# A two-layer decoder trunk with a product-key expert stage: 16 more tokens take gathered expert rows, and the gates come from one product

## The chip, the cores and the metric

The kernel runs on one core of one Trainium2 chip. The metric is device time in microseconds (us) of one launch. The engines are TensorE (PE, with its weight loads PEld), VectorE (DVE), ScalarE (ACT), GpSimd (POOL) and SyncE (SP), and 16 DMA engines move data.

## The reference

Two layers (`DEPTH = 2`), 512 tokens of width 1024, all float32. Each layer has a token mixer (retention beside a gated linear recurrence), cross-attention into 256 memory tokens, and an expert stage, here called PEER; a final norm closes it. The change touches the expert stage alone, which is:

```python
def _peer(x, g_ffn, w_pq, sub_k1, sub_k2, peer_u, peer_v):
    hf = _rmsnorm(x, g_ffn).reshape(N, D)
    q = (hf @ w_pq).reshape(N, PEER_HEADS, PEER_KEY_DIM)
    ...
    v1, i1 = lax.top_k(s1, K)
    v2, i2 = lax.top_k(s2, K)
    cand = (v1[..., :, None] + v2[..., None, :]).reshape(N, PEER_HEADS, K * K)
    vals, ci = lax.top_k(cand, K)
    ...
    idx = (e1 * PEER_KEYS + e2).reshape(N, PEER_HEADS * K)
    gates = jax.nn.softmax(vals, axis=-1).reshape(N, PEER_HEADS * K)
    ...
    ub = jnp.take(peer_u, ib, axis=0)
    act = jax.nn.gelu(jnp.einsum('tkd,td->tk', ub, xb).astype(jnp.float32))
    vb = jnp.take(peer_v, ib, axis=0)
    out = jnp.einsum('tk,tkd->td', (gb * act).astype(vb.dtype), vb)
```

Eight heads pick 16 experts each, so a token uses 128 of the 16,384 experts. An expert is a row of `peer_u` and a row of `peer_v`, 1024 numbers each.

## The kernel before, in words

**Two ways to do an expert.** Of the 512 tokens, the first `TD = 384` are done densely: all 16,384 experts are computed for them, in `NK = 128` units of 128 experts, and a gate that is zero for the experts not chosen selects. The last 128 tokens, one per partition, are done by rows: for each of the 128 places k of a token's list, a gather (an indirect DMA on POOL) brings 128 rows of 1024, one per partition.

**Products.** A float32 product is made of three float32r products of split halves (`mm3`): the weight w is cast by ACT to its high part `wh` (L200), DVE subtracts to get the low part `wl` (L202). `pull` and `weights` keep two weights ahead; `w` has 4 buffers, `wh` and `wl` 3. The weights of all stages come in one order, so the first weight of the next layer's mixer follows V's last one.

**Stages of an expert layer.** First queries and keys (`keys`, `top16`): DVE finds the best 16 of each half, and L853 turns each index into a number `idf`. Then **U**: unit j multiplies `peer_u`'s weight with the tokens (24 matmuls of 384 columns, L216 to L218), ACT applies gelu into `ag`, and SP stores `acts`. Three generators are fed between the units, each by a credit: `routes` (route by route in the order `RORD`: candidates, top 16, look-ups L905 and L907, softmax), `scatter` (gates), and `rows_u` (the gathered rows of U, with `XPACE` per unit). `scatter` spreads the gates of four tokens at a time over all 128 x 128 experts: DVE makes one-hot rows, ACT scales them, PE multiplies. Two of four groups use split halves (256 columns, L963, then a copy and DVE's addition L967), two a plain float32 product (128 columns, L971). `rows_u` multiplies each gathered row with `hrow` on DVE and sums along it (L782).

Then **V**: for unit j, `wv` = activation times gate (L1066), split into `ws` (L222, L223), and 24 products into eight accumulators `out`, one bank each, which are held for the whole stage. Units run in groups of 8 from the last group to the first (`v_order`); the last two units of the last group (j = 6 and 7) are held back. `rest` first finishes `rows_u`, then runs `rows_v`: gather into `rv` (4 buffers, L795), then DVE adds it, times `wrow`, to `yrow` (L800). It gets a credit of `VPACE = 1.75` per unit against 1.3 per gather, and whatever is left runs behind the last unit. At the end, for each of the eight accumulators, L1080 adds `yrow` transposed, then the two held units are added, and L1084 adds the result to `x`.

Each engine runs its instructions in program order, as the kernel's scheduler has arranged them; a waiting instruction holds up all those behind it on its engine.

Of the kernel before, what the change touches and what calls it, by code (L numbers as in the profile page):

```python
# [19 lines left out]
D = 1024  # L20
T = 512
# [12 lines left out]
TD = 384  # L34
# [4 lines left out]
GVN = 2  # L39
# [3 lines left out]
RORD = [*range(TD // 128, TT), *range(TD // 128)]  # L43
# [14 lines left out]
XPACE = 0.8  # L58
# [95 lines left out]
def trunk(ctx: ExitStack, tc: tile.TileContext, A, out, dbg=None):  # L154
# [107 lines left out]
    nc.scalar.copy(identr, ident)  # L262

# [497 lines left out]
    def peer(l):  # L761
        acts = dram.tile([NK // GRP, 128, GRP, TD], F32, name=f"acts{l}")
        gd = dram.tile([NK // GRP, 128, NTB, GRP, TB], F32, name=f"gates{l}")
        NG = T // 128 - TD // 128
        left = ExitStack()
        gp = left.enter_context(tpool(name=f"pg{l}", bufs=1))
        if NG:
            hrow = gp.tile([128, D], F32, name="hrow")
            arow = gp.tile([128, 128], F32, name="arow")
            grow = gp.tile([128, 128], F32, name="grow")  # L770
            irow = gp.tile([128, 2, 128], I32, name="irow")
            wrow = gp.tile([128, 128], F32, name="wrow")
# [3 lines left out]
        def rows_u():  # L776
            for k in range(PH * K):
                r = gp.tile([128, D], F32, name="rows", bufs=3)
                nc.gpsimd.indirect_dma_start(out=r, out_offset=None, in_=A["peer_ur"].rearrange("l e d -> (l e) d"),  # L779
                                             in_offset=bass.IndirectOffsetOnAxis(ap=irow[:, 0, k:k + 1], axis=0))  # L780
                s = gp.tile([128, D], F32, name="prod", bufs=1)
                nc.vector.scalar_tensor_tensor(s, r, 1.0, hrow, op0=OP.mult, op1=OP.mult, accum_out=arow[:, k:k + 1])  # L782
                yield 1.3
                if k % 32 == 31:
                    ks = slice(k - 31, k + 1)
                    nc.scalar.activation(wrow[:, ks], arow[:, ks], AF.Gelu_apprx_tanh)
                    nc.vector.tensor_mul(wrow[:, ks], wrow[:, ks], grow[:, ks])

        def rows_v(vp):
            yrow = vp.tile([128, D], F32, name="yrow")  # L790
            ysum.append(yrow)
            pv = A["peer_v"].rearrange("l j n d -> (l j n) d")
            for k in range(PH * K):
                r = vp.tile([128, D], F32, name="rv", bufs=RVB)
                nc.gpsimd.indirect_dma_start(out=r, out_offset=None, in_=pv,  # L795
                                             in_offset=bass.IndirectOffsetOnAxis(ap=irow[:, 1, k:k + 1], axis=0))
                if k == 0:
                    nc.vector.tensor_scalar(yrow, r, wrow[:, k:k + 1], None, op0=OP.mult)
                else:
                    nc.vector.scalar_tensor_tensor(yrow, r, wrow[:, k:k + 1], yrow, op0=OP.mult, op1=OP.add)  # L800
                yield 1.3
# [8 lines left out]
        with tpool(name=f"pr{l}", bufs=1) as rt, tpool(name=f"ph{l}", bufs=1) as hp, tpool(name=f"pps{l}", bufs=4, space=PS) as psum, \  # L810
# [14 lines left out]
            def token_rows():  # L825
                for c0 in range(0, DC, 4):
                    tr = psm.tile([128, 4, 128], F32, name="sm")
                    for i in range(4):
                        for k in range(2):
                            nc.tensor.matmul(tr[:, i], lhsT=h[c0 + i][:, 1 - k, TD:T], rhs=identr, start=k == 0,  # L830
                                             stop=k == 1)
                    nc.scalar.copy(hrow[:, c0 * 128:(c0 + 4) * 128], tr.rearrange("p c i -> p (c i)"))
# [8 lines left out]
            with tpool(name=f"pk{l}", bufs=1) as kp:  # L841
                def keys(hd, i, q, sk):
# [6 lines left out]
                    for t in range(TT):  # L849
                        wk = kp.tile([128, NK], F32, name="wk", bufs=2)  # L850
                        idx = kp.tile([128, K], U32, name="idx", bufs=2)
                        top16(val[i][t][:, hd], idx, s[:, t], wk)
                        nc.vector.scalar_tensor_tensor(idf[i][t][:, hd], idx, (NK if i == 0 else 1.0) / IDS,  # L853
                                                       C("first") if i == 0 else C("iota")[:, 0:K],
                                                       op0=OP.mult, op1=OP.add)

                for c in range(2 * PH):
# [12 lines left out]
                    if c == 3 and NG:  # L870
                        token_rows()
                drain()

# [4 lines left out]
            def route(t):  # L878
# [3 lines left out]
                ohs = [big[:, o:o + K * NC_].rearrange("p (k c) -> p k c", k=K)  # L882
                       for o in (2 * PH * NC_, 2 * PH * NC_ + K * NC_)]
# [19 lines left out]
                for hd in range(PH):  # L903
                    oh = ohs[hd % 2]
                    nc.vector.tensor_sub(oh, cid[:, hd, None, :].to_broadcast([128, K, NC_]),  # L905
                                         cf[:, hd, :, None].to_broadcast([128, K, NC_]))
                    nc.vector.tensor_reduce(ee[:, hd], oh, axis=AX.X, op=OP.min, apply_absolute_value=True)  # L907
                    yield 1.8
# [15 lines left out]
                if t * 128 >= TD:  # L924
                    nc.vector.tensor_copy(grow, ex[:, 2])
                    base = float(l * NK * NK)
                    nc.vector.tensor_scalar(irow[:, 0], ee.rearrange("p h k -> p (h k)"), IDS, base, op0=OP.mult,  # L927
                                            op1=OP.add)
# [239 lines left out]
```

## Time and profile before

| | us |
| --- | --- |
| median of 3 runs | 3853.55 |
| lowest and highest run | 3851.89, 3855.34 |
| the profiled execution | 3855.28 |
| its span (first to last instruction) | 3853.2 |
| PE busy in the span | 3801.3 (99%) |
| DVE busy | 2999.6 (78%) |
| ACT busy | 1900.1 (49%) |
| POOL busy | 734.3 (19%) |
| moved by DMA | 877.06 MB |

The span is the profiled execution without what lies around it (2.1 us). Busy time of PE counts matmuls as they overlap in the pipeline, so its share says that PE had work, not that it ran at its peak. The mean granted clock of PE was 0.995. In layer 1 the U stage runs from about 808 to 1390 us, V from there to 1917 us.

### The profile page before, as it was taken

To read this page: it belongs to the slowest core of one execution; us is meant where nothing else is said; L and a number is where in the kernel's file an instruction comes from. 1 tells how busy PE (TensorE), PEld (TensorE's weight loads), DVE (VectorE), ACT (ScalarE), POOL (GpSimd) and SP (SyncE) were. 2 spreads that over 40 slices of the span, in tenths; PEclk is the share of its full clock that TensorE was granted. 3 is DMA by queue.
4 is the path that set the end of the run, shared out by engine and by line. 5 is a ranking of instruction groups with operands and counts; after the bars stand their busy time and mean duration, and the time that the engine had idled before them with its cause. 6 is when DMAs were issued, how large, how long until landed. Compare 5 with 4: busy or idle time off the path is not lost.

```text
span 3853.2 us, 56299 instructions
## 1 busy us (share of the span) xinstructions
PE 3801.3 (99%) x20636; PEld 3535.2 (92%) x20636; DVE 2999.6 (78%) x5556; ACT 1900.1 (49%) x3531; POOL 734.3 (19%) x517
## 2 busy tenths in 40 slices
PE   8999999999999999999999999999999999999998
PEld 7888888899999999999978888878999999999998
DVE  7449665999989968777854596659999898687877
ACT  5336444336778843333343363543367788333333
POOL 0000000013233323333200000000232333233432
PEclk9999999999999999999999999999999999999999
DMA  4222342268999989999722223322689999899995
GB/s 150 82 87 95 104 134 69 83 208 317 309 319 348 335 325 338 345 346 346 269 82 77 93 94 104 131 67 88 232 308 312 319 350 315 332 348 342 345 346 213
DMA packets 313476, 877.06 MB, mean 228 GB/s; under 512 B 24945, under 2 KB 131569, under 8 KB 305265
## 3 DMA queue, kind: packets, MB, share of 16 engines
q1 hardware_dynamic: 239472, 605.01, 44.3%
q0 software_dynamic: 73728, 268.47, 19.8%
q8 instruction: 162, 2.65, 0.3%
q14 instruction: 114, 0.93, 0.1%
HBM read 776.13 MB, written 97.26 MB: 227 GB/s over the span
## 4 chain that ended last, share of the span: by engine, by line
PE 88%; DVE 8%; DMA 2%; issue 1%; ACT 1%; POOL 0%; SPq 0%; DVEq 0%; ACTq 0%; POOLq 0%
PE acc L216 18%; PE acc L218 18%; PE acc L217 18%; PE out L216 9%; PE out L217 9%; PE out L218 9%; PE sm L971 2%; DVE wl L202 2%; DMA rows<-peer_ur,irow 1%; PE sm L963 1%; DVE wk L837 1%; DVE idx L839 1%; DVE idx L836 1%; DVE val L838 1%; DVE val L835 1%
## 5 line engine op out<-in xcount | busy, mean ns | idle before, releaser
L200 ACT CAST wh<-w 128x1024 fp32r<-128x1024 f32 x768 | 802.0, 1049 | 1028.0 <-PE acc L217 662.7
L202 DVE TENSOR_TENSOR wl<-w,wh 128x1024 fp32r<-128x1024 f32 x768 | 935.1, 1218 | 338.9 <-ACT wh L200 315.5
L779 POOL DMA_INDIRECT rows<-peer_ur,irow x256 | 360.9, 1410 | 2354.9 <-DVE irow L927 1687.6
L216 PE MATMUL acc<-hf,wh 128*128 128x384 f32 (+1 forms) x2256 | 777.2, 344 | 7.3 <-DVE hf L223 6.1
L218 PE MATMUL acc<-hf,wl 128*128 128x384 f32 (+1 forms) x2256 | 775.9, 345 | 5.9 <-DVE wl L202 5.8
L217 PE MATMUL acc<-hf,wh 128*128 128x384 f32 (+1 forms) x2256 | 774.0, 343 | 0.0
L216 PE MATMUL out<-ws,wh 128*128 128x384 f32 x2048 | 687.6, 336 | 6.3 <-DVE ws L223 6.3
L217 PE MATMUL out<-ws,wh 128*128 128x384 f32 x2048 | 685.9, 335 | 0.0
L218 PE MATMUL out<-ws,wl 128*128 128x384 f32 x2048 | 575.8, 335 | 0.0
L216 PE MATMUL acc<-a,wh 128*128 128x512 f32 x1280 | 507.4, 397 | 15.9 <-ACT wh L200 10.5
L795 POOL DMA_INDIRECT rv<-peer_v,irow x256 | 373.0, 1457 | 716.6 <-DVE yrow L800 609.7
L217 PE MATMUL acc<-a,wh 128*128 128x512 f32 x1280 | 505.1, 395 | 0.0
L218 PE MATMUL acc<-a,wl 128*128 128x512 f32 x1280 | 503.8, 394 | 0.1
L216 PEld LDWEIGHTS acc<-hf,wh 128*128 128x128 f32 x2256 | 425.4, 189 | 17.9 <-DVE hf L223 8.7
L218 PEld LDWEIGHTS acc<-hf,wl 128*128 128x128 f32 x2256 | 425.1, 189 | 17.2 <-DVE wl L202 8.8
L217 PEld LDWEIGHTS acc<-hf,wh 128*128 128x128 f32 x2256 | 425.4, 189 | 7.8
L222 ACT CAST ws<-wv 128x384 fp32r<-128x384 f32 x256 | 131.1, 512 | 537.8 <-PE out L218 268.9
L216 PEld LDWEIGHTS out<-ws,wh 128*128 128x128 f32 x2048 | 385.8, 188 | 6.9 <-DVE ws L223 6.9
L217 PEld LDWEIGHTS out<-ws,wh 128*128 128x128 f32 x2048 | 385.7, 188 | 0.0
L953 ACT ACTIVATE ob<-oab,pg 128x128 fp32r<-128x128 f32 (+1 forms) x1152 | 357.2, 393 | 38.6 <-DVE oab L947 37.7
L218 PEld LDWEIGHTS out<-ws,wl 128*128 128x128 f32 x2048 | 375.9, 188 | 0.0
L800 DVE SCALAR_TENSOR_TENSOR yrow<-rv,wrow,yrow 128x1024 f32<-128x1024 f32 x254 | 324.5, 1278 | 50.9 <-DMA rv<-peer_v,irow 50.9
(291 smaller groups left out, 5186.5 us busy)
## 6 DMA issues: line engine op xcount, KB each, us to landing
w<-peer_u SPq DMA_DIRECT2D x256, 512.0 KB, 5.8
w<-peer_v SPq DMA_DIRECT2D x256, 512.0 KB, 6.3
gates<-stage SPq DMA_DIRECT2D x48, 1024.0 KB, 8.6
gg<-gates SPq DMA_DIRECT2D x30, 1536.0 KB, 9.0
acts<-ag SPq DMA_DIRECT2D x56, 768.0 KB, 6.2
ar<-acts SPq DMA_DIRECT2D x28, 1536.0 KB, 13.7
w<-w_f SPq DMA_DIRECT2D x80, 512.0 KB, 3.3
w<-w_t SPq DMA_DIRECT2D x32, 512.0 KB, 3.3
```

The source lines that it names most:

```text
L200: nc.scalar.copy(wh, w)
L202: nc.vector.tensor_sub(wl, w, wh.bitcast(F32))
L216: nc.tensor.matmul(acc, lhsT=lh, rhs=rl, start=start, stop=False)
L217: nc.tensor.matmul(acc, lhsT=lh, rhs=rh, start=False, stop=False)
L218: nc.tensor.matmul(acc, lhsT=ll, rhs=rh, start=False, stop=stop)
L222: nc.scalar.copy(dst[:, 0], src)
L779: nc.gpsimd.indirect_dma_start(out=r, out_offset=None, in_=A["peer_ur"].rearrange("l e d -> (l e) d"), in_offset=bass.IndirectOffsetOnAxis ...
L795: nc.gpsimd.indirect_dma_start(out=r, out_offset=None, in_=pv, in_offset=bass.IndirectOffsetOnAxis(ap=irow[:, 1, k:k + 1], axis=0))
L800: nc.vector.scalar_tensor_tensor(yrow, r, wrow[:, k:k + 1], yrow, op0=OP.mult, op1=OP.add)
L835: nc.vector.max(v[:, 0:8], src)
L953: nc.scalar.activation(ob[:, i, k % 2], oh[:, 2 * i + 1].bitcast(F32), AF.Copy, scale=pg[:, k, t0 + i:t0 + i + 1])
L971: nc.tensor.matmul(g[:, i], lhsT=oh[:, 2 * i], rhs=ob[:, i, 0], start=True, stop=True)
```

## The change

**Tokens.** `TX = 16`: the dense tokens are 368, and tokens 368 to 383 join the gathered ones. These 16 are held eight times over the 128 partitions, partition 16 g + e holding token e for the heads' part g, so that 16 more gathers of 128 rows in U and 16 in V do their 128 experts each. A product with `pick` replicates their routes, `half` selects each partition's own 16 places, token rows are replicated by ACT copies (`hx`) and transposed by 16 products per layer, and at the end a product with `fold` (16 columns) sums the eight copies. So `hrow`, `arow`, `grow`, `irow`, `wrow`, `yrow` become pairs, and `rows_u` and `rows_v` go over 128 and then 16 places.

**Gates.** `GVN = 0`: all groups of four tokens use the plain float32 product.

**Order and batches.** Routes go in the order 3, 2, 0, 1 (before 3, 0, 1, 2), and gates in 2, 0, 1; `XPACE` goes from 0.8 to 1.3. The index conversions are done by `numbers(t)`, two instructions for a route instead of one for each key and head. Look-ups take two heads at a time. In V, `wv` and `ws` are made for two units at once (736 columns). `rows_u` writes its product in place.

```diff
 TB = 16
-TD = 384
+TX = 16
+TD = 384 - TX
+NX = 128 // TX
...
-GVN = 2
+GVN = 0
...
-RORD = [*range(TD // 128, TT), *range(TD // 128)]
+RORD = [3, 2, 0, 1]
...
-XPACE = 0.8
+XPACE = 1.3
...
+    fold = keep.tile([128, TX], F32, name="fold")
+    nc.vector.tensor_reduce(fold, ident.rearrange("p (g e) -> p e g", g=NX), axis=AX.X, op=OP.add)
+    half = keep.tile([128, 2], F32, name="half")
...
+    pick = keep.tile([128, NX, TX], F32, name="pick")
...
         def rows_u():
...
+            for i, n in enumerate((PH * K, TX)):
+                while not routed[RORD[i]]:
+                    yield
+                for k in range(n):
+                    r = gp.tile([128, D], F32, name="rows", bufs=3)
...
         def rows_v(vp):
...
+            for i, n in enumerate((PH * K, TX)):
+                yrow = vp.tile([128, D], F32, name=f"yrow{i}")
+                ysum.append(yrow)
+                for k in range(n):
+                    r = vp.tile([128, D], F32, name="rv", bufs=RVB)
...
-                        top16(val[i][t][:, hd], idx, s[:, t], wk)
-                        nc.vector.scalar_tensor_tensor(idf[i][t][:, hd], idx, (NK if i == 0 else 1.0) / IDS,
-                                                       C("first") if i == 0 else C("iota")[:, 0:K],
-                                                       op0=OP.mult, op1=OP.add)
+                        top16(val[i][t][:, hd], idf[i][t][:, hd].bitcast(U32), s[:, t], wk)
...
-                for hd in range(PH):
-                    oh = ohs[hd % 2]
...
+                for hd in range(0, PH, 2):
+                    nc.vector.tensor_sub(oh, cid[:, hd:hd + 2, None, :].to_broadcast([128, 2, K, NC_]),
+                                         cf[:, hd:hd + 2, :, None].to_broadcast([128, 2, K, NC_]))
...
+                if t == RORD[1]:
+                    rep = psm.tile([128, 3, PH * K], F32, name="sm")
+                    nc.tensor.matmul(rep.rearrange("p i k -> p (i k)"), lhsT=pick.rearrange("p g e -> p (g e)"),
+                                     rhs=ex.rearrange("p i k -> p (i k)"), start=True, stop=True)
...
+                    nc.vector.tensor_copy(grow[1], own[:, 2])
+                    places(irow[1], own[:, 0], own[:, 1])
...
-                wv = vp.tile([128, TD], F32, name="wv", bufs=2)
...
-                ws = vp.tile([128, 2, TD], F32R, name="ws", bufs=max(3, NCM))
-                split(ws, wv)
-                pend.append((weights("v", l, j, ahead=1 if j == GRP - 1 else 2), ws))
+                if i % 2 == 0:
+                    act = ar[:, i:i + 2] if kept < 0 else last[kept // 4][:, i % 4:i % 4 + 2]
+                    wv = vp.tile([128, 2, TD], F32, name="wv", bufs=2)
...
+                    ws = vp.tile([128, 2, 2, TD], F32R, name="ws", bufs=2)
+                    split(ws, wv)
+                pend.append((weights("v", l, j, ahead=1 if j == GRP - 1 else 2), ws[:, :, i % 2]))
...
             for c in range(DC):
-                if NG:
-                    nc.tensor.matmul(acc[c][:, TD:T], lhsT=ysum[0][:, c * 128:(c + 1) * 128], rhs=ident, start=False,
+                for i, (ts, to) in enumerate(((slice(T - 128, T), ident), (slice(TD, T - 128), fold))):
+                    nc.tensor.matmul(acc[c][:, ts], lhsT=ysum[i][:, c * 128:(c + 1) * 128], rhs=to, start=False,
                                      stop=False)
                 for j in range(GRP - NCM, GRP):
                     products(j, pend[j - GRP + NCM], [c])
```

**Order on DVE at the end of V, layer 1, before.** `yrow` is the accumulator of the gathered rows, `wl` the low part of a weight, `wv` and `ws` the weighted activations; the last `wl` belongs to the next layer's mixer.

```order
L800 SCALAR_TENSOR_TENSOR yrow<-rv,wrow,yrow 128x1024
L1066 TENSOR_TENSOR wv<-ar_17947,gg_17945 128x384
L800 SCALAR_TENSOR_TENSOR yrow<-rv,wrow,yrow 128x1024
L202 TENSOR_TENSOR wl<-w,wh 128x1024
L223 TENSOR_TENSOR ws<-wv,ws 128x384
L1066 TENSOR_TENSOR wv<-ar_17947,gg_17945 128x384
L202 TENSOR_TENSOR wl<-w,wh 128x1024
L223 TENSOR_TENSOR ws<-wv,ws 128x384
L202 TENSOR_TENSOR wl<-w,wh 128x1024
L223 TENSOR_TENSOR ws<-wv,ws 128x384
L202 TENSOR_TENSOR wl<-w,wh 128x1024
L1084 TENSOR_TENSOR x_67<-out_13172,x_67 128x512
```

The last two of the 128 sums (L800) stand ahead of V's last two weights and of the next mixer's first.

**The same place now** (the lines have moved: L204 for L202, L225 for L223, L815 for L800, L1133 for L1084). `yrow_12739` is the accumulator of the 128 tokens, `yrow_16251` that of the 16.

```order
L815 SCALAR_TENSOR_TENSOR yrow_12739<-rv,wrow_5141,yrow_12739 128x1024
L813 TENSOR_SCALAR yrow_16251<-rv,wrow_5146 128x1024
L204 TENSOR_TENSOR wl<-w,wh 128x1024
L815 SCALAR_TENSOR_TENSOR yrow_16251<-rv,wrow_5146,yrow_16251 128x1024
L225 TENSOR_TENSOR ws<-wv,ws 128x736
L815 SCALAR_TENSOR_TENSOR yrow_16251<-rv,wrow_5146,yrow_16251 128x1024
L204 TENSOR_TENSOR wl<-w,wh 128x1024
L815 SCALAR_TENSOR_TENSOR yrow_16251<-rv,wrow_5146,yrow_16251 128x1024
L204 TENSOR_TENSOR wl<-w,wh 128x1024
L815 SCALAR_TENSOR_TENSOR yrow_16251<-rv,wrow_5146,yrow_16251 128x1024 x12
L1133 TENSOR_TENSOR x_67<-out_12696,x_67 128x512
```

The last sum of the first accumulator stands ahead of three weights and the next mixer's first one; twelve sums of the second stand behind all of these, ahead of the additions to `x`. In layer 2, where no stage's weight follows, thirteen sums stand behind V's last weight.

**Order on PE at the same place, before.** `out` are the eight accumulators; the products with `ident` add the gathered rows, those with `ws` are the held units.

```order
L1080 MATMUL out_13172<-ident,yrow 128x128
L216 MATMUL out_13172<-ws,wh 128x384
L217 MATMUL out_13172<-ws,wh 128x384
L218 MATMUL out_13172<-ws,wl 128x384
L1080 MATMUL out_13173<-ident,yrow 128x128
L216 MATMUL out_13173<-ws,wh 128x384
L217 MATMUL out_13173<-ws,wh 128x384
L218 MATMUL out_13173<-ws,wl 128x384
```

Each accumulator takes its gathered rows and then its share of the held units.

**The same place now** (L218 to L220 for L216 to L218, L1129 for L1080).

```order
L1129 MATMUL out_12702<-ident,yrow_12739 128x128
L1129 MATMUL out_12703<-ident,yrow_12739 128x128
L1129 MATMUL out_12696<-fold,yrow_16251 128x16
L218 MATMUL out_12696<-ws,wh 128x368
L219 MATMUL out_12696<-ws,wh 128x368
L220 MATMUL out_12696<-ws,wl 128x368
L218 MATMUL out_12696<-ws,wh 128x368
L219 MATMUL out_12696<-ws,wh 128x368
L220 MATMUL out_12696<-ws,wl 128x368
L1129 MATMUL out_12697<-fold,yrow_16251 128x16
```

All eight products of the first gathered accumulator go ahead, and the first product with `fold`, which reads the second one, stands ahead of all 48 products of the held units.

## Rows read from the trace of the kernel before

**Rows 1.** The page: busy time of each engine, its share of the span, instructions
```profile
PE 3801.3 (99%) x20636; PEld 3535.2 (92%) x20636; DVE 2999.6 (78%) x5556; ACT 1900.1 (49%) x3531; POOL 734.3 (19%) x517
```

**Rows 2.** Windows: length, busy PE, PEld, DVE, ACT, POOL; PE clock, DMA share, GB/s
```profile
808.00:1090.00 282.00, 278.30 (x1652) 276.97 (x1651) 272.15 (x588) 172.24 (x380) 84.12 (x62) 0.99 0.87 299
1150.00:1330.00 180.00, 180.00 (x1126) 180.00 (x1125) 164.72 (x221) 154.75 (x410) 66.56 (x46) 1.00 1.00 347
1400.00:1850.00 450.00, 450.00 (x2598) 450.00 (x2598) 364.94 (x436) 158.10 (x217) 163.05 (x112) 1.00 0.91 345
1900.00:1950.00 50.00, 43.34 (x199) 37.72 (x198) 29.18 (x40) 21.14 (x32) 0.00 (x0) 0.86 0.31 101
```

**Rows 3.** Timeline of PE: start, duration; 256 columns, then 384 columns
```profile
509.76 0.28 PE L216 MATMUL acc<-mn,wh 128*128 128x256 f32 x1
...
510.72 0.28 PE L218 MATMUL acc<-mn,wl 128*128 128x256 f32 x1
...
1200.55 0.34 PE L217 MATMUL acc<-hf,wh 128*128 128x384 f32 x1
...
1201.94 0.34 PE L216 MATMUL acc<-hf,wh 128*128 128x384 f32 x1
```

**Rows 4.** Groups by line and form on PE; last a piece of the chain
```profile
L216 PE MATMUL acc<-hf,wh 128*128 128x384 f32 x2048 | 693.8, 339 | 1.2 <-ACT wh L200 1.2
...
L963 PE MATMUL sm<-ob,oab 128*128 128x256 f32 x384 | 105.0, 282 | 0.0
L971 PE MATMUL sm<-ob,oab 128*128 128x128 f32 x768 | 104.0, 275 | 0.4 <-ACT ob L953 0.4
...
694.31 1.78 PE sm L845 x16
```

**Rows 5.** Groups by line and form on DVE: count, busy us, mean ns, idle before
```profile
L782 DVE SCALAR_TENSOR_TENSOR prod<-rows,hrow 128x1024 f32<-128x1024 f32 x256 | 311.5, 1217 | 28.8 <-DMA rows<-peer_ur,irow 27.9
...
L967 DVE TENSOR_TENSOR stage<-sm,stage 128x256 f32<-128x256 f32 x192 | 75.3, 415 | 2.4 <-ACT stage L966 2.2
...
L853 DVE SCALAR_TENSOR_TENSOR idf<-idx,cst 128x16 f32<-128x16 uint32 x128 | 20.0, 158 | 0.0
```

**Rows 6.** Timeline of DVE, ends of V, layers 1 and 2; in brackets idle time
```profile
1894.97 1.27 DVE L800 SCALAR_TENSOR_TENSOR yrow<-rv,wrow,yrow 128x1024 f32<-128x1024 f32 x1
1896.17 1.22 DVE L202 TENSOR_TENSOR wl<-w,wh 128x1024 fp32r<-128x1024 f32 x1
...
1908.33 1.23 DVE L202 TENSOR_TENSOR wl<-w,wh 128x1024 fp32r<-128x1024 f32 x1 [2.46 <-ACT wh L200]
...
3824.52 1.23 DVE L202 TENSOR_TENSOR wl<-w,wh 128x1024 fp32r<-128x1024 f32 x1 [2.47 <-ACT wh L200]
```

**Rows 7.** Tile yrow, PE: ns min/median/max, first and last start
```profile
L1080 PE MATMUL out<-ident,yrow x32: 271/274/275, 1907.2 to 3836.6; 128*128 128x128 f32 x32
```

**Rows 8.** Tile rv: issues on POOL, and from issue to landing
```profile
L795 POOL DMA_INDIRECT rv<-peer_v,irow x256: 935/1012/3756, 1363.4 to 3804.4; - x128
...
DMA to landing us min/median/max: 4.1/9.2/14.2
```

**Rows 9.** Timeline of POOL late in V of layer 2
```profile
3779.05 1.01 POOL L795 DMA_INDIRECT rv<-peer_v,irow  x1 [1.79 <-DVE yrow L800]
...
3783.52 3.75 POOL L795 DMA_INDIRECT rv<-peer_v,irow  x1 [0.65 <-DVE yrow L800]
...
3795.66 1.01 POOL L795 DMA_INDIRECT rv<-peer_v,irow  x1 [1.79 <-DVE yrow L800]
```

**Rows 10.** Timeline of PE after V of layer 1, first products of the next mixer
```profile
1921.42 0.77 PE L216 MATMUL acc<-a,wh 128*128 128x512 f32 x1 [3.80 <-DVE a L370]
...
1927.10 0.50 PE L217 MATMUL acc<-a,wh 128*128 128x512 f32 x1
...
1927.67 0.39 PE L216 MATMUL acc<-a,wh 128*128 128x512 f32 x1
1927.90 0.39 PE L217 MATMUL acc<-a,wh 128*128 128x512 f32 x1
```

More of the change, by code (lines that the diff above doesn't have):

```diff
@@ L774, in peer @@
+        for i, n in enumerate((PH * K, TX)):
+            hrow.append(gp.tile([128, D], F32, name=f"hrow{i}"))
+            arow.append(gp.tile([128, n], F32, name=f"arow{i}"))
+            grow.append(gp.tile([128, n], F32, name=f"grow{i}"))
+            irow.append(gp.tile([128, 2, n], I32, name=f"irow{i}"))
+            wrow.append(gp.tile([128, n], F32, name=f"wrow{i}"))
         ysum = []
         def rows_u():
[L777 to L787, printed above, removed]
@@ L869, in peer, with numbers @@
                     tasks.append(keys(hd, i, q, sk))
-                    if c == 3 and NG:
-                        token_rows()
+                    if c == 3:
+                        token_rows(kp)
                 drain()
+            def numbers(t):
+                for i, first in enumerate((C("first"), C("iota")[:, 0:K])):
+                    nc.vector.scalar_tensor_tensor(idf[i][t], idf[i][t].bitcast(U32), (NK if i == 0 else 1.0) / IDS,
+                                                   first[:, None, :].to_broadcast([128, PH, K]),
+                                                   op0=OP.mult, op1=OP.add)
             pp = es.enter_context(tpool(name=f"pu{l}", bufs=1))
@@ L985, in scatter @@
             def scatter():
-                for t in range(TD // 128):
+                for t in RORD[1:]:
                     pend = None
-                    for t0 in range(t * 128, (t + 1) * 128, 4):
+                    end = min((t + 1) * 128, TD)
+                    for t0 in range(t * 128, end, 4):
                         while not routed[t]:
@@ L1000, in scatter @@
                     collect(*pend)
-                    put((t + 1) * 128 // TB - 1, pend[-1])
+                    put(end // TB - 1, pend[-1])
                 gates[NK // GRP - 1] = gate_group(gp, "big", NK // GRP - 1)
-            rows = rows_u() if NG else iter(())
+            rows = rows_u()
             todo, groups = routes(), scatter()
@@ L1016, in peer @@
                     rc -= next(todo, 9.0)
-                if routed[0]:
+                if routed[RORD[1]]:
                     gc += GPACE
@@ L1021, in peer @@
                         next(groups, DONE)
-                if routed[TT - 1] and NG:
+                if routed[RORD[0]]:
                     xc += XPACE
@@ L1040, in rest @@
             yield from rows
-            if NG:
-                yield from rows_v(vp)
+            yield from rows_v(vp)
         credit = 0.0
```

103 lines of the change are left out of this document (62 added, 41 removed).

## The prediction, made before the changed kernel had run

> **What bounds the kernel now.** I read the page's busy shares first, then busy time by windows, then the starts of single matmuls, and last the order of VectorE and TensorE at the end of the expert stage. TensorE (PE) is busy for 99% of the span [rows 1]. In a window of the U stage and in one of the V stage it is busy for the whole window [rows 2]. So a matmul made shorter there shortens the span, as long as nothing else takes over. The next two candidates are close. VectorE (DVE) is busy for 272 of 282 us early in U [rows 2], and the 16 DMA engines have a busy share of 1.00 late in U and 0.91 in V. PE's "busy" overlaps itself (a 384-column matmul shows 339 ns [rows 4]), so I price matmuls by the distance between starts: eight steps take 0.96 us at 256 columns and 1.39 us at 384 [rows 3]. That is 120 and 174 ns, or 0.42 ns a column.
>
> **The sum, both layers.** It is made against the profiled execution (3855.28 us; its span is 3853.2), which lies 1.7 above the median 3853.55.
>
> *A. Narrower products.* U and V each take 128 units of 24 matmuls in each of two layers, 12,288 in all (the 2048 of one line in [rows 4] are a third of U's). Each streams 368 columns instead of 384, which lies between the two measured widths: 16 x 0.42 = 6.7 ns. **-82.6 us.**
>
> *B. Gates from one product.* A group of four tokens was either four 256-column products of split halves or four plain fp32 products. 384 and 768 records [rows 4] make 96 groups of each kind, since an fp32 product leaves two records. Sixteen fp32 records take 1.78 us [rows 4], so a plain group costs 8 x 0.111 = 0.89 us and a split one 4 x 0.120 = 0.48. Now there are 184 groups, all plain: 163.8 against 131.5. **+32.2 us.** The DVE additions of split groups go with this (192 of 415 ns [rows 5]), but PE pays more.
>
> *C. Small products.* 32 transposes of the 16 replicated tokens (128 columns, 0.066 us by the slope) are 2.1. Two 384-column fp32 products that replicate the routes cost at most three 128-column ones each (0.22), together 1.3. Sixteen 16-column products that fold the result lie between nothing and 0.22 each; nearer to nothing by width, I take 0.07, or 1.1. **+4.5 us.**
>
> *D. The end of V.* This is the term that decides. 144 gathered tiles are summed in V, still about one per unit. In the old order all 128 sums stand ahead of the last two weights of V. In the new order of layer 1, 12 sums into the second accumulator stand behind the subtraction of the next stage's first weight. That subtraction waits for a weight buffer that the product of unit j = 5 frees. Call the end of that product P (1907.2 in the trace [rows 7]). The subtraction started at 1908.33 [rows 6], so it is done at P + 2.3. The sums follow, each 1.20 us from start to start (1894.97 to 1896.17 [rows 6]). Four of their gathers fit into the four buffers and have been issued before, which brings us to P + 7.1. Each of the other eight needs a buffer that the sum four places ahead frees, then an issue by GpSimd, then the landing. A cycle of four is about 0.35 to the issue, the landing and 1.3 for the sum with its semaphore. The landing takes 4.1 us at least and 9.2 in the middle of a loaded V [rows 8]; with only a few weights in flight I take 5.7. That is 7.4 us for four, 1.85 each, and the last sum ends at P + 21.9.
> PE has only the eight products of the first accumulator (1.8 us) before it needs the second one, because the two held units stand behind it. It idles for 20.1 us. After such a wait it also starts slow: after 3.8 us of idleness thirteen 512-column steps took 5.68 us, up to 1927.10, where those behind took 0.23 each [rows 10]. That is the 1.2 GHz level against the 2.4, and 2.7 us lost; the granted clock of that window is 0.86 [rows 2]. Layer 1: 22.8.
> In layer 2 no stage follows, and 13 sums stand behind V's own last weight. Its subtraction started at 3824.52 [rows 6], and P was about 3827.5: in layer 1 V's last weight stands one unit (24 x 0.1735 = 4.16 us) ahead of the row at 1908.33, so 3.0 ahead of P. So the sums start at P - 1.8, four are done at P + 3.0, nine more at P + 19.6, and PE idles for 17.8: 20.5 with the clock. **+43.3 us** for both layers. The bounds: DVE alone sets the pace (12 and 13 sums of 1.20: 17.6 and 14.7, together 32.3), or the gathers come as slowly as the seven issued at 3779.05 to 3795.66 [rows 9], 2.77 us each: 30.2 and 28.8, together 59.0. Those issues were spaced by demand too, so I stay nearer to the lower end.
> The Trainium skill, page "SBUF — State Buffer", section "SBUF: two separate sides", says that VectorE and GpSimd share one port pair as an exclusive lock, so that GpSimd cannot write a gather's descriptors while certain VectorE operations run. The trace agrees in kind: issues took 0.94 to 3.76 us [rows 8], and by the longest the sum would be that of the slow end. The page "DMA: Bandwidth & Descriptors", section "Anatomy of one DMA — SWDGE (gpsimd) path", fits a gather of 512 KB as 2.0 us plus bytes over 436 GB/s, an estimate of 3.2 us; no landing here was below 4.1, so the rows decide, but by it the sum would be near the fast end.
>
> *E. What may hide or show.* Early in U, where DVE is nearly full, the change takes away 128 small index conversions (158 ns [rows 5]) and half of the additions of the first gate groups. It adds about 12 gathered rows per layer (1.22 us each [rows 5], and a short accumulator read) and the places of the 16 tokens. By the counts in the order this is some 6 us less for DVE per layer; PE gets some 7 us lighter over the same units. The stalls there stay: 0. The ends: all of what this window lost goes (282 - 278.3 and 1% of clock, 6.5 per layer), or as much comes on top. Late in U, 40 weights now go with 56 gathered rows and 59 gate groups instead of 53 and 50. The bytes grow from 69 to 73 MB (0.52 MB a weight or a gather, 0.26 a group's gates, 0.19 a unit's activations), but through B PE also takes 213 instead of 201 us, and the rate stays near the 347 GB/s of the window [rows 2]: 0. At the switch from U to V, PE's short wait is a chain through ScalarE's last activation, the cast and DVE's subtraction, which stays; the cast is now a pair's, while the gates are loaded earlier: 0. In V the batches of two units take fixed cost off DVE, which has room there (365 of 450 us [rows 2]), so no gain. Gathered rows arrive a little more often than PE needs weights: **+2 us** for late ones.
>
> Sum: -82.6 + 32.2 + 4.5 + 43.3 + 2 = -0.6, which is 3854.7 against the profiled execution, and **3853.0 as a median.** A measurement of this kernel can tell 0.2%, 7.7 us, from no change.
>
> **The rivals.**
> *R1, slower: the issue of gathers paces the end of V.* Place: the eight and nine late gathers. Price: (2.77 - 1.85) x 17 = 15.7, 3869. It decides once a gather takes over 2.3 us on average in that row of sums (17 x 0.49 = 8.3 more puts the time 0.2% above the old). For it: an issue of 3.75 us among seven gathers [rows 9]. Against it: the sums there stood between other DVE work.
> *R2, slower: DMA becomes the bound of V.* Per layer it has to move 128 weights and about 136 gathers of 0.52 MB and 29 loads of 1.5 MB, 182 MB in the 512 us of 3072 steps of 0.167: 356 GB/s, where the window shows 345 [rows 2]. If 345 were all it can do, 15.5 us more per layer, 3884. Against it: the share there is 0.91, and PE never waited.
> *R3, faster: the end of V is cheap.* If most gathers have landed or land in 4.1 us with quick issues, DVE alone sets the pace: -11.0, 3842.
> *R4, faster: the early U stage loses its stalls*, since keys and routing cost DVE fewer instructions: 6.5 per layer less, 3840.
> *R5: the change doesn't do what it says.* If a matmul's step had a floor at 174 ns, A would be nothing: 3936. The 120 ns step at 256 columns [rows 3] speaks against it.
>
> **How the numbers follow.** Forecast (D as reckoned, within 7.7 of 3853.55) 0.43; R1 0.24; R2 0.08; R3 0.14; R4 0.09; R5 0.02. So faster 0.23, same 0.43, slower 0.34. The forecast alone reaches from 3846 to 3861; with most of R1, R3 and R4 the range is 3838 to 3877, which leaves out R5, R2 and the far ends of R1.
>
> **What would show it.** The step of a 368-column matmul at 167 ns, 184 plain gate groups of 0.89 us, and no group of 256-column gate products. At each V's end a row of 12 or 13 sums 1.2 to 2.8 us apart, PE idle for some 20 and 18 us ahead of the first product with the second accumulator, and then matmuls at the lower clock. PE busy late in U and in V as before. I am wrong if that idle time is under 14 or over 27 us, if PE waits for weights inside V, or if U's early stalls move by more than 5 us per layer.

## The result, and the profile after

The changed kernel takes 3921.33 us (median of 4 runs, 3919.93 to 3922.73) against 3853.45 for the kernel before (4 runs): ratio 1.0175, interval 1.016 to 1.019. The forecast was 3853, no change. The profiled execution took 3919.93 us, its span is 3918.2, 65.0 longer than before.

The first part of the page after, for [rows 1]:

```profile
PE 3789.4 (97%) x21024; PEld 3514.3 (90%) x21024; DVE 2976.9 (76%) x5053; ACT 1754.2 (45%) x2905; POOL 847.6 (22%) x581
```

Windows of the kernel after, columns as in [rows 2]; the last row is the end of V in layer 1:

```profile
808.00:1090.00 282.00, 274.83 (x1697) 271.04 (x1696) 265.41 (x553) 146.31 (x288) 114.37 (x72) 1.00 0.89 308
1150.00:1330.00 180.00, 180.00 (x1219) 180.00 (x1218) 153.62 (x180) 136.71 (x333) 66.70 (x47) 1.00 1.00 348
1400.00:1850.00 450.00, 440.58 (x2571) 439.05 (x2571) 348.82 (x322) 146.82 (x159) 153.95 (x108) 0.98 0.89 341
1920.00:1940.00 20.00, 0.00 (x0) 0.00 (x0) 11.86 (x10) 0.00 (x0) 9.00 (x8) 0.50 0.79 298
```

Late in U PE is busy throughout, as before. In V it no longer is: 440.6 of 450 us where [rows 2] had all 450. DMA's share there fell from 0.91 to 0.89, so it is not a fuller DMA. At the end of V PE does nothing for 20 us, at a granted clock of 0.50 (1.2 GHz).

Timeline of PE after, in U, for [rows 3] and the last of [rows 4]:

```profile
1201.15 1.05 PE L1018 MATMUL sm<-ob,oab 128*128 128x128 f32 x8
1201.96 0.42 PE L218 MATMUL acc<-hf,wh 128*128 128x368 f32 x1
1202.21 0.33 PE L219 MATMUL acc<-hf,wh 128*128 128x368 f32 x1
...
1204.05 0.33 PE L218 MATMUL acc<-hf,wh 128*128 128x368 f32 x1
...
1205.55 0.33 PE L218 MATMUL acc<-hf,wh 128*128 128x368 f32 x1
```

Nine steps take 1.50 us: 167 ns a matmul, as forecast. The gate group takes 1.06 us until the second step behind it, less one step 0.89. Terms A and B are right.

So the time was lost in waits. From the starts of single instructions I take three stretches per layer: U from its first to its last product, V from the low-part subtraction of its first weight to that of its last, and the end from there to the ninth subtraction of the next layer (in layer 2, to the end of the span).

| us, layers 1 and 2 | U | V | end of V |
| --- | --- | --- | --- |
| before | 608.2, 609.3 | 532.7, 534.7 | 66.3, 28.7 |
| after | 611.3, 613.8 | 535.4, 532.7 | 93.1, 54.2 |
| forecast for after | 603.8, 604.9 | 513, 515 | 89.1, 49.2 |

Against the forecast U is 16 us too long in both layers together, V 40 and the end 9.

**V.** Timeline of ScalarE after, at one of the places where PE stalls:

```profile
1533.23 0.81 ACT L224 CAST ws<-wv 128x736 fp32r<-128x736 f32 x1 [3.14 <-PE out L220]
1541.34 0.80 ACT L224 CAST ws<-wv 128x736 fp32r<-128x736 f32 x1 [7.30 <-PE out L220]
1542.05 2.94 ACT L202 CAST wh<-w 128x1024 fp32r<-128x1024 f32 x3
```

of PE behind it, and of PE's clock there (window, columns as above):

```profile
1543.14 0.43 PE L218 MATMUL out<-ws,wh 128*128 128x368 f32 x1 [1.88 <-ACT wh L202]
...
1544.14 0.51 PE L218 MATMUL out<-ws,wh 128*128 128x368 f32 x1
1544.45 0.51 PE L219 MATMUL out<-ws,wh 128*128 128x368 f32 x1
```

```profile
1543.00:1546.00 3.00, 2.86 (x11) 2.86 (x12) 2.98 (x4) 2.00 (x3) 0.00 (x0) 0.61 0.20 49
```

Two casts of a pair (736 columns) stand in a row. The second waits 7.30 us for one of the two `ws` buffers, until the products of an earlier pair end (`PE out L220`). Three weight casts stand behind it, though they wait for no load; they run at 1542.05, and PE waits for them, 1.88 us. Then it steps 0.31 instead of 0.167 us for twelve matmuls (granted clock 0.61 in the window, 1.2 GHz in its steps), which loses as much again: 3.7 us in all. This happens five times in each layer, near 1543, 1611, 1680, 1748 and 1816 us in the first.

Casts in a row are not enough by themselves. Before the change two single casts stood in a row too, here on ScalarE, and PE had no wait inside V:

```profile
1545.50 0.51 ACT L222 CAST ws<-wv 128x384 fp32r<-128x384 f32 x1 [2.73 <-issue]
1549.66 0.51 ACT L222 CAST ws<-wv 128x384 fp32r<-128x384 f32 x1 [3.65 <-PE out L218]
```

**The end of V.** PE after, both layers:

```profile
1914.36 1.95 PE L1129 MATMUL out<-ident,yrow 128*128 128x128 f32 x16
1941.04 0.61 PE L1129 MATMUL out<-fold,yrow 128*128 128x16 f32 x2 [24.73 <-DVE yrow L815]
...
3889.50 0.61 PE L1129 MATMUL out<-fold,yrow 128*128 128x16 f32 x2 [21.06 <-DVE yrow L815]
```

VectorE and GpSimd at the same place in layer 1, for [rows 6, 9]:

```profile
1915.47 1.22 DVE L204 TENSOR_TENSOR wl<-w,wh 128x1024 fp32r<-128x1024 f32 x1 [1.25 <-ACT wh L202]
1916.61 2.60 DVE L815 SCALAR_TENSOR_TENSOR yrow<-rv,wrow,yrow 128x1024 f32<-128x1024 f32 x2
1920.03 1.28 DVE L815 SCALAR_TENSOR_TENSOR yrow<-rv,wrow,yrow 128x1024 f32<-128x1024 f32 x1 [0.82 <-DMA rv<-peer_v,irow]
1921.75 1.28 DVE L815 SCALAR_TENSOR_TENSOR yrow<-rv,wrow,yrow 128x1024 f32<-128x1024 f32 x1 [0.44 <-DMA rv<-peer_v,irow]
1927.20 5.25 DVE L815 SCALAR_TENSOR_TENSOR yrow<-rv,wrow,yrow 128x1024 f32<-128x1024 f32 x4 [4.16 <-DMA rv<-peer_v,irow]
1934.00 1.28 DVE L815 SCALAR_TENSOR_TENSOR yrow<-rv,wrow,yrow 128x1024 f32<-128x1024 f32 x1 [1.56 <-DMA rv<-peer_v,irow]
1936.42 1.29 DVE L815 SCALAR_TENSOR_TENSOR yrow<-rv,wrow,yrow 128x1024 f32<-128x1024 f32 x1 [1.14 <-DMA rv<-peer_v,irow]
1938.38 2.60 DVE L815 SCALAR_TENSOR_TENSOR yrow<-rv,wrow,yrow 128x1024 f32<-128x1024 f32 x2 [0.68 <-DMA rv<-peer_v,irow]
```

```profile
1918.16 1.86 POOL L810 DMA_INDIRECT rv<-peer_v,irow  x1 [2.73 <-DVE yrow L815]
1920.33 1.80 POOL L810 DMA_INDIRECT rv<-peer_v,irow  x1 [0.30 <-issue]
1922.43 1.42 POOL L810 DMA_INDIRECT rv<-peer_v,irow  x1 [0.30 <-issue]
1924.15 0.94 POOL L810 DMA_INDIRECT rv<-peer_v,irow  x1 [0.30 <-issue]
1928.75 1.86 POOL L810 DMA_INDIRECT rv<-peer_v,irow  x1 [3.66 <-DVE yrow L815]
```

From issue to landing, of the first four of these gathers:

```profile
DMA to landing us min/median/max: 6.5/7.5/8.9
```

The row of twelve sums is there as forecast, each behind its gather (`DMA rv`). From 1923.03, the end of the fourth, to 1940.98, the end of the twelfth, a sum took 2.24 us on average.

### The profile page after: what moved, and what is told of

It is laid out like the page before. It is cut to its first block, busy times and chain, and to the rows that moved or that the text cites. A ratio compares the mean times of both kernels' runs of the same rounds, so it can differ in the third digit from the quotient of the medians.

```text
span 3918.2 us, 55531 instructions
## 1 busy us (share of the span) xinstructions
PE 3789.4 (97%) x21024; PEld 3514.3 (90%) x21024; DVE 2976.9 (76%) x5053; ACT 1754.2 (45%) x2905; POOL 847.6 (22%) x581
## 3 DMA queue, kind: packets, MB, share of 16 engines
q1 hardware_dynamic: 235344, 597.15, 42.6%
## 4 chain that ended last, share of the span: by engine, by line
PE 75%; DVE 10%; issue 6%; DMA 5%; POOL 3%; ACT 1%; SPq 0%; POOLq 0%; DVEq 0%; ACTq 0%
PE acc L218 15%; PE acc L220 15%; PE acc L219 15%; PE out L218 8%; PE out L219 8%; PE out L220 8%; DMA rows<-peer_ur,irow 3%; PE sm L1018 3%; DVE wl L204 2%; POOL rows L792 2%; DMA rv<-peer_v,irow 1%; POOL rv L810 1%; DVE rows L795 1%; DVE wk L862 1%; DVE idf L861 1%
## 5 line engine op out<-in xcount | busy, mean ns | idle before, releaser
L202 ACT CAST wh<-w 128x1024 fp32r<-128x1024 f32 x768 | 797.5, 1048 | 1223.9 <-PE acc L219 726.9
L204 DVE TENSOR_TENSOR wl<-w,wh 128x1024 fp32r<-128x1024 f32 x768 | 936.7, 1220 | 374.2 <-ACT wh L202 350.3
L792 POOL DMA_INDIRECT rows<-peer_ur,irow x288 | 436.8, 1517 | 2312.8 <-DVE ci L864 1692.6
L220 PE MATMUL acc<-hf,wl 128*128 128x368 f32 (+1 forms) x2256 | 762.7, 339 | 14.4 <-DVE wl L204 14.3
L218 PE MATMUL acc<-hf,wh 128*128 128x368 f32 (+1 forms) x2256 | 764.5, 339 | 7.4 <-DVE hf L225 6.1
L219 PE MATMUL acc<-hf,wh 128*128 128x368 f32 (+1 forms) x2256 | 762.0, 338 | 0.0
L218 PE MATMUL out<-ws,wh 128*128 128x368 f32 x2048 | 689.1, 336 | 25.2 <-ACT wh L202 19.1
L219 PE MATMUL out<-ws,wh 128*128 128x368 f32 x2048 | 686.9, 335 | 0.0
L810 POOL DMA_INDIRECT rv<-peer_v,irow x288 | 410.4, 1425 | 723.0 <-DVE yrow L815 640.0
L220 PE MATMUL out<-ws,wl 128*128 128x368 f32 x2048 | 542.9, 332 | 0.0
L218 PE MATMUL acc<-a,wh 128*128 128x512 f32 x1280 | 506.3, 396 | 15.7 <-ACT wh L202 10.3
L220 PE MATMUL acc<-a,wl 128*128 128x512 f32 x1280 | 503.9, 394 | 0.1
L220 PEld LDWEIGHTS acc<-hf,wl 128*128 128x128 f32 x2256 | 424.4, 188 | 27.9 <-DVE wl L204 19.7
L218 PEld LDWEIGHTS acc<-hf,wh 128*128 128x128 f32 x2256 | 424.9, 188 | 18.5 <-DVE hf L225 8.7
L218 PEld LDWEIGHTS out<-ws,wh 128*128 128x128 f32 x2048 | 392.4, 192 | 28.9 <-ACT wh L202 22.2
L795 DVE SCALAR_TENSOR_TENSOR rows<-rows,hrow 128x1024 f32<-128x1024 f32 x288 | 350.1, 1220 | 57.1 <-DMA rows<-peer_ur,irow 56.8
L219 PEld LDWEIGHTS out<-ws,wh 128*128 128x128 f32 x2048 | 392.6, 192 | 0.0
L815 DVE SCALAR_TENSOR_TENSOR yrow<-rv,wrow,yrow 128x1024 f32<-128x1024 f32 x284 | 364.5, 1283 | 22.4 <-DMA rv<-peer_v,irow 21.1
L220 PEld LDWEIGHTS out<-ws,wl 128*128 128x128 f32 x2048 | 371.9, 190 | 0.0
L224 ACT CAST ws<-wv 128x736 fp32r<-128x736 f32 x128 | 103.1, 807 | 466.1 <-PE out L220 306.9
```

The lines of the kernel that those rows point to most:

```text
L202: nc.scalar.copy(wh, w)
L204: nc.vector.tensor_sub(wl, w, wh.bitcast(F32))
L218: nc.tensor.matmul(acc, lhsT=lh, rhs=rl, start=start, stop=False)
L219: nc.tensor.matmul(acc, lhsT=lh, rhs=rh, start=False, stop=False)
L220: nc.tensor.matmul(acc, lhsT=ll, rhs=rh, start=False, stop=stop)
L224: nc.scalar.copy(dst[:, 0], src)
```

## The experiments

Each run's profile gives the stretches of the table above; ratios are to the kernel before on the same chip.

**One: V unit by unit.**

```diff
-                if i % 2 == 0:
-                    wv = vp.tile([128, 2, TD], F32, name="wv", bufs=2)
+                wv = vp.tile([128, TD], F32, name="wv", bufs=2)
...
-                    ws = vp.tile([128, 2, 2, TD], F32R, name="ws", bufs=2)
+                ws = vp.tile([128, 2, TD], F32R, name="ws", bufs=max(3, NCM))
```

> The changed kernel, but V's weighted activations and their split are made unit by unit again (368 columns, three buffers of ws). Theory (the cast of a pair waits for one of two pair buffers and holds up the weight casts behind it on ScalarE): the stalls of 3.8 us inside V go, about 40 us of both layers, so about 3881 us; the idle time ahead of the first product with the second accumulator stays at 20 to 25 us per layer. Rival (V is bound by DMA or by the gathers now, and the pair cast only shows it): V keeps its length, within 10 us of 3921.

Measured: 3915.59, ratio 1.0149 (1.0132 to 1.0166); V 529.9 and 530.0. A miss: the time is the rival's, and the pair by itself is not the cause. ScalarE of this run shows why:

```profile
1543.28 0.50 ACT L224 CAST ws<-wv 128x368 fp32r<-128x368 f32 x1 [2.56 <-PE out L220]
1547.35 0.50 ACT L224 CAST ws<-wv 128x368 fp32r<-128x368 f32 x1 [3.57 <-PE out L220]
1551.37 0.50 ACT L224 CAST ws<-wv 128x368 fp32r<-128x368 f32 x1 [3.52 <-PE out L220]
1551.77 1.04 ACT L202 CAST wh<-w 128x1024 fp32r<-128x1024 f32 x1
```

Three single casts stand in a row, each waiting for a product, and the weight's cast behind. It costs 1.8 us instead of 3.7, since PE's wait of 1.58 us was followed by steps of 0.167 us, at eight places in a layer instead of five.

**Two: also six buffers for V's gathers** (`RVB = 6`).

> As the run before, and six buffers instead of four for V's gathered rows, so that the order has no sum behind the last weight of V. Theory (the idle time at the end of V is the sums left over, each behind a gather that waits for a buffer): 45 to 53 us less than the run before, about 3832. Rival (the gathers come at a rate that DMA sets, so V is stretched instead): PE idles inside V, and the gain over the run before is under 20 us.

Measured: 3879.41, ratio 1.0058 (1.0041 to 1.0075). The end of V falls to 67.4 and 30.9, as before the change, so the left-over sums were that loss. V took 535.7 and 541.8, with eleven waits of 1.58 to 2.9 us for ScalarE's weight casts in each layer. The gain over run one, 36 us, lies between the theory's and the rival's. From 1500 to 1800 us V moved 397 to 402 GB/s, at a DMA share of 1.00, so 345 was no limit, and rival R2 falls.

**Three: half of the gates split again** (`GVN = 2`).

> The changed kernel with two of four gate groups made of split halves again (256-column products and an addition on VectorE). Theory (term B: a plain group costs PE 0.41 us more): half of the 184 groups, 38 us less matmul time on PE, of which VectorE's additions give back a part early in U; 3885 to 3895. Rival (U is held by VectorE and by the gathers, PE's share there is not its limit): under 15 us less, above 3906.

Measured: 3913.09, ratio 1.0142 (1.0125 to 1.0159): the rival's figure in time, but not by its mechanism. U fell to 586.4 and 586.0, and PE then waited at the switch to V:

```profile
1379.81 2.08 PE L1018 MATMUL sm<-ob,oab 128*128 128x128 f32 x8 [1.75 <-ACT ob L1000]
1396.46 0.67 PE L218 MATMUL out<-ws,wh 128*128 128x368 f32 x1 [14.57 <-DVE ws L225]
```

Eight gate groups, half of them split, had been put behind U's last product in the order, and then their store and the load of `big` had to pass: 38.9 and 42.6 us from U's last product to V's first, instead of 3.4.

**Four: U's gathered rows at 0.8 per unit** (`XPACE = 0.8`).

> The changed kernel with the gathered rows of U given 0.8 instead of 1.3 per unit. Theory (the stalls early in U are VectorE waiting for a gathered row with a weight's subtraction behind it, since rows come too densely): U loses 6 to 10 us less per layer, and V's end has 7 and 9 sums left instead of 12 and 13, another 8 us per layer: 3890 to 3900. Rival (U's stalls come from the new order of the routes and the replicated tokens): U keeps its length, 3905 to 3912.

Measured: 3900.63, ratio 1.0114 (1.0097 to 1.0131). U 605.7 and 611.1, V 529.0 and 538.6, end 86.7 and 46.1: of the 22 us between the profiled executions, 14.5 came from the end of V, where fewer sums were left. U gave 5.6 and 2.7 us, less than the theory's 6 to 10, so the time is near its range without its reason.

**Five: ScalarE's casts of V in program order**, nothing else.

```diff
-        nc.scalar.copy(wh, w)
+        hi = nc.scalar.copy(wh, w)
+        if key[0] == "v":
+            tc.keep_in_program_order(hi)
...
-                    split(ws, wv)
+                    tc.keep_in_program_order(nc.scalar.copy(ws[:, 0], wv))
+                    nc.vector.tensor_sub(ws[:, 1], wv, ws[:, 0].bitcast(F32))
```

> The changed kernel, with ScalarE's casts of V alone (weights and pairs of weighted activations) held in the order in which the program writes them; nothing else. Theory (V's stalls are a question of order on ScalarE: two pair casts in a row, the second waiting for a buffer that a product must free, with the casts of the next weights behind it): the stalls of 3.8 us go, four or five per layer, V's 127 weights take 514 to 518 us instead of 535 and 533, and the time falls by 30 to 40 us to about 3885. The first run fits this too: its single casts stood three in a row and cost 2.0 us each time. Rival (a resource: DMA or VectorE in V): V keeps 527 us or more, and the time stays above 3905.

Measured: 3881.69, ratio 1.0074 (1.0057 to 1.0091); V 517.2 and 517.5. ScalarE now alternates, and no pair cast has another in front of it:

```profile
1501.74 1.05 ACT L202 CAST wh<-w 128x1024 fp32r<-128x1024 f32 x1 [2.97 <-PE out L221]
1502.70 0.80 ACT L1120 CAST ws<-wv 128x736 fp32r<-128x736 f32 x1
1505.75 1.06 ACT L202 CAST wh<-w 128x1024 fp32r<-128x1024 f32 x1 [2.25 <-PE out L221]
1509.78 1.05 ACT L202 CAST wh<-w 128x1024 fp32r<-128x1024 f32 x1 [2.97 <-PE out L221]
1510.74 0.80 ACT L1120 CAST ws<-wv 128x736 fp32r<-128x736 f32 x1
```

So the stalls are shown to be ScalarE's order: the same work, buffers and transfers, and none of the five in a layer is left. One wait per layer is new, early in V, 5.6 and 3.9 us, for a weight that had not landed.

The stretch makes too much of the gain. With the casts in program order the first weight's subtraction stands 4.7 us ahead of V's first product, where it stood 10.1 ahead, so V seems 5.4 us shorter. PE tells it without that, from V's first product to the first product with `ident`; first the changed kernel, whose last row stands above (1914.36), then this run:

```profile
1386.45 0.55 PE L218 MATMUL out<-ws,wh 128*128 128x368 f32 x1 [3.06 <-DVE ws L225]
```

```profile
1389.34 0.43 PE L220 MATMUL out<-ws,wh 128*128 128x368 f32 x1 [2.22 <-DVE ws L1121]
...
1904.38 1.95 PE L1132 MATMUL out<-ident,yrow 128*128 128x128 f32 x16
```

That is 527.9 and now 515.0 us (525.1 and 515.3 in layer 2), where 3024 steps of 0.167 make 504. So V gave 12.9 and 9.8 us, 23 of the 42 between the two profiled executions. Most of the rest, 17, came from the end of V, which fell to 84.5 and 45.6, since eight and nine sums were left over in this order. The expectation did not have that: its time was met in part by luck. In runs seven to ten and thirteen, too, the stretch makes V about 6 us shorter than PE does.

**Six: the products with `fold` behind the held units** (two loops over the accumulators instead of one).

> The changed kernel, with the eight products of the second accumulator moved behind all products of the held units. Theory (PE waits for the last sum in both cases, but now with 48 products of 0.167 us done before): the wait ahead of the first product with fold falls from 24.7 and 21.1 us to about 17 and 13, 16 us less, about 3905. Rival (PE's wait is given back at the lower clock or in the additions to x): under 8 us less.

Measured: 3908.54, ratio 1.0147 (1.013 to 1.0164).

```profile
1936.06 3.60 PE L1133 MATMUL out<-fold,yrow 128*128 128x16 f32 x16 [17.87 <-DVE yrow L815]
...
3877.36 3.59 PE L1133 MATMUL out<-fold,yrow 128*128 128x16 f32 x16 [12.60 <-DVE yrow L815]
3887.42 0.56 PE L347 MATMUL acc<-ones,sqs 128*128 128x1 f32 x2 [6.46 <-DVE sqs L340]
```

The waits are as expected (17.87 and 12.60), their gain is not: the end of V fell by 7.5 and 3.1 only, and the rest of the 12.8 us less came from elsewhere. All additions to `x` now come after the wait, in a row, and in layer 2 PE waits 6.46 us for the squares behind them.

**Seven: one and two, with five's order.**

> V unit by unit with six gather buffers (as the second run), and the casts of V in the order of the program. Theory (order and left-over sums are two separate costs): no stalls in V and no sums left over, 24 us per layer less than the second run: its ratio to the kernel before falls from 1.006 to about 0.994, 3832 on a chip where the kernel before takes 3853. Rival (with all gathers inside V and no stalls, 186 MB in 512 us or 364 GB/s, DMA sets the end of V): V takes 525 us or more and the ratio stays above 1.0.

Measured: 3851.22, ratio 0.9991 (0.9981 to 1.0001); V 524.2 and 522.9, end 63.5 and 31.1. Half a miss. One wait per layer is left near V's start:

On ScalarE:

```profile
1413.84 1.04 ACT L202 CAST wh<-w 128x1024 fp32r<-128x1024 f32 x1 [16.48 <-DMA w<-peer_v]
```

on SyncE's queue:

```profile
1386.18 0.82 SPq L824 DMA_DIRECT2D gg<-gates  x2
1387.04 0.91 SPq L1111 DMA_DIRECT2D ar<-acts  x2
1389.40 27.09 SPq L200 DMA_DIRECT2D w<-peer_v  x5
```

and on PE:

```profile
1416.65 0.68 PE L220 MATMUL out<-ws,wh 128*128 128x368 f32 x1 [8.59 <-DVE ws L1119]
```

The weight's load, issued at 1389.40, stood on SP behind four loads of gates and activations of 1.5 MB, with five gathers issued since 1383.4 besides, and landed 24.3 us after its issue.

**Eight: as seven, with `XPACE = 0.8`.**

> As the run before, with the gathered rows of U at 0.8 per unit. Theory (rows that come too densely make VectorE wait for a gather with a weight's subtraction behind it): U 3 to 6 us shorter per layer, 3822 to 3828. Rival (the shorter U of the fourth run came with more rows left for V): no difference of 3 us from the run before.

Measured: 3824.79, ratio 0.9923 (0.9906 to 0.994). U 606.8 and 608.5, V 512.7 and 513.4, end 61.9 and 30.3. From V's first product to the first with `ident` PE took 511.5 and 512.2 us, some 8 above the 504 that its steps make. U is 6 and 3 us shorter, as the theory has it, but 21 of the 31 us between the profiled executions of runs seven and eight came in V, where the wait near the start is gone. That was not foreseen, so the time is in its range by luck. The trace shows why it went: in this order V's first six gathers were issued from 1364 to 1371 and had landed by 1380.6, ahead of the four big loads, and the next one was issued at 1394.4. So the weight issued behind those loads landed after 14.3 us instead of 24.3.

**Nine: as eight, look-ups one head at a time.**

> As the eighth run, with the look-ups of the routes one head at a time again (800 columns instead of 1600). Theory (U's stalls are late subtractions on VectorE, and an instruction of 1.8 us holds one up longer than one of 1.0): U 2 to 6 us shorter per layer, 3815 to 3820 on this scale. Rival (gathered rows and gates set U's pace, look-ups are a small part): U the same within 2 us, the ratio to the kernel before within 0.002 of 0.992.

Measured: 3825.56, ratio 0.9921 (0.9904 to 0.9937); U 609.3 and 610.1, 2.5 and 1.6 us longer than in run eight. In the main the rival: look-ups don't set U.

**Ten: as eight, `XPACE = 0.6`.**

> As the eighth run, with the gathered rows of U at 0.6 per unit. Theory (rows that come too densely hold up weights in U): U another 2 to 5 us shorter per layer. Rival (the rows have to be done by U's end or they land in V): U the same, and V 2 to 10 us longer per layer.

Measured: 3818.87, ratio 0.9901 (0.9884 to 0.9917), not told apart from eight; U 611.5 and 608.1, V 510.1 and 512.3. In this profile U isn't shorter and V isn't longer, so neither theory shows; but the profiled execution took 3827.74 us, the longest of the four (the shortest 3813.81), so a U that is a few us shorter at the median isn't excluded. It has the lowest median here, and like eight it beats both kernels.

**Eleven: look-ups one head at a time, alone.**

> The changed kernel with the look-ups one head at a time and nothing else: the edit stands in U, but the scheduler's order of V comes out otherwise. In that order two pair casts stand in a row, with the next weights' casts behind, at one place per layer instead of five, and 6 and 8 sums stand behind the last weight instead of 12 and 13. Theory (order alone makes the loss in V): V's 127 weights take 517 to 521 us instead of 535 and 533, PE's wait at the end is about 10 to 13 us instead of 24.7 and 21.1, and the time is 3865 to 3875. Rival (a resource): V keeps 527 us or more.

Measured: 3883.42, ratio 1.0069 (1.0052 to 1.0086); V 523.2 and 524.0, PE's waits at the end 14.1 and 10.2 us. An edit in U moved V by 12 and 9 us and its end by 9 and 10, through the order. V stayed 2 and 3 us above the range, with three waits of 1.1 to 2.2 us in layer 1 and two of 1.9 and 2.5 in layer 2 where one each was foreseen, and the time 8 us.

**Twelve and thirteen: U with half of the gathers, and with half of the sums.**

> As the eighth run, but every second gather of U is left out (its sum uses the row before again), so VectorE's work is the same and 38 MB per layer less are moved. Theory (U is held by the landing of gathered rows and weights, DMA share 0.9 to 1.0): U falls from 607 and 608 us to below 602. Rival (VectorE's own work holds U): U stays within 3 us.

> As the eighth run, but every second sum of U is made over 16 columns only (it leaves out the rest), so all gathers stay and VectorE has 72 x 1.1 = 79 us less to do per layer. Theory (VectorE's own work holds U): U falls from 607 and 608 us to below 602, towards its 594 us of matmul steps. Rival (the landing of gathers and weights holds it): U stays within 3 us.

Measured: 3875.85 (ratio 1.0057, 1.0034 to 1.0079) and 3825.74 (0.9923, 0.9894 to 0.9952). Without half of the gathers U took 592.4 and 595.1, but 13 gate groups stood behind its last product and the switch took 35 us, as in run three. Counting U's own products and gates at their steps, what is left over in U is 9.7 and 12.4 us there, 12.3 and 12.9 with half of the sums, 12.5 and 14.2 in run eight, 17.0 and 19.5 after the change, 9.6 and 10.8 before. So VectorE's sums don't hold U. For the gathers it stays undecided, since the 2 to 3 us that went without half of them went together with the 13 gate groups.

## Why the prediction was wrong

**A and B were right** (167 ns, 0.89 us a group). C was small and too low: the stretch from the first query product to U, with the transposes, is 1.8 us longer per layer, 3.6 for both where 2.1 stood, and a product with `fold` adds 0.23 us between the matmuls beside it (1948.34 to 1948.90 in the trace, less two steps), not 0.07.

**The step that failed is E's sentence on V**: "In V the batches of two units take fixed cost off DVE, which has room there, so no gain", with 2 us for late rows. It looked at VectorE alone. The order of ScalarE's casts came out otherwise too, and that order, which the prediction did not read, made PE wait: V was 22 and 18 us longer than the forecast's 513 and 515, most of it five stalls of 3.7 us per layer. The prediction's own sign of being wrong, "if PE waits for weights inside V", came. Run five takes out all ten stalls by the order alone; V gains 12.9 and 9.8 us by it, since one new wait per layer came. What in the change moved the order is open: run one undid the pairs and had eight such places per layer, and run eleven moved it by U's look-ups alone. The Trainium skill, page "PSUM — Partial Sum Buffer", section "Engine vs sequencer instructions", says that ScalarE's queue is strictly first in, first out; the rows of ScalarE above show what that costs when a cast whose buffer isn't free stands ahead of one whose data are there.

**D, the end of V, was right in mechanism and short in size.** PE waited 24.73 and 21.06 us (20.1 and 17.8 forecast); with the slow clock behind it the end grew by 26.8 and 25.5 instead of 22.8 and 20.5. The landing was taken as 5.7 us for all late gathers, and the first four as landed in time. In layer 1 the four issued from 1918.16 to 1924.15 landed 8.9 to 6.5 us after their issue; beside them stood loads of the next stage, the last of which landed at 1926.9. The next four took 5.2 to 6.1. So a late sum took 2.24 us there, not 1.85. In layer 2, where no stage follows, the landings took 5.1 to 6.3 us as forecast, and a sum 1.98; most of the excess there lies in the first four sums, of which the fourth waited for its gather too. So the landing is the term that was short; that the loads beside it made it so is likely, but no run shows it. R1's issues had a smaller part: GpSimd's issues in the four rows up to 1924.15 took 1.86 to 0.94 us, one behind the other, and three of the four started 1.1 us after their buffer was free instead of 0.35; of the port that the Trainium skill gives GpSimd and VectorE in common (page "SBUF — State Buffer", section "SBUF: two separate sides") no run here shows what part it had. Run two, without sums left over, is without the term.

**E's "0" for U was wrong by about 8 us per layer**: what is left over beside the steps grew from 9.6 and 10.8 to 17.0 and 19.5. PE's waits in U grew from 3.7 and 3.8 to 8.1 and 11.0 us, 5.0 and 9.2 of them for a weight's subtraction on VectorE, so the sentence "the stalls there stay" is the step that failed in U. The runs leave what is left over at 10 to 23, with 1 to 8 us between the layers of one kernel; slower rows (runs four and eight) take some of it, look-ups and sums none. What makes those subtractions late stays open, and so does how a change of rows alone, at the old width, would fare.

**R2** fell with run two (397 to 402 GB/s in V). **R3** did not come, and **R4**'s gain came the other way round.

## What to carry to other kernels

Where a scheduler sets each engine's order, read the order on every engine that feeds the busy one, not only on the one that an edit relieves: casts that were ready behind a cast that wasn't cost ten stalls of 3.7 us here, and holding them in program order took all ten away, for 23 us net. A row of work left over at a stage's end made PE wait 25 and 21 us here, and two more buffers took that away, though V grew by 6 and 12 us with them (run two against run one). A stretch between two instructions is only comparable where both stand at the same place in the order, so check it against the engine that is busy. And an edit can move the order of a stage that it doesn't touch, so a change is timed with that order held before it is judged.

## What was not expected of the hardware

Half of each stall in V was the clock: the wait of 1.88 us ahead of 1543.14 was followed by 3.4 us at the 1.2 GHz level, where waits of 1.58 us in run one were not. The length of the wait doesn't settle it: one of 2.17 us in run eight was followed by steps of 0.167 us at a granted clock of 1.00.

```profile
1683.39 0.44 PE L220 MATMUL out<-ws,wh 128*128 128x368 f32 x1 [2.17 <-DVE ws L1119]
```

Fewer transfers came with a slower kernel: with half of U's gathers left out the time rose from 3824.8 to 3875.9 us, since in the order of that kernel gate groups stood behind U's last product. V moved 397 to 402 GB/s in run two, where before the change 345 GB/s had looked like a ceiling at a DMA share of 0.91.
